# Raw LoRA weights fetched two pieces ahead into a two-buffer tile, in a one-core hybrid RWKV-7 / FoX block

## The chip, the cores and the metric

The kernel runs on one core of one Trainium2 chip. The metric is the device time of one execution in microseconds (us). The kernel before took 854.08 us, the median of three runs (852.34, 854.08 and 855.10).

In the text, PE is TensorE (PEld its weight loads), DVE is VectorE, ACT is ScalarE, POOL is GpSimd, and SP is SyncE, whose queue issues nearly all loads. L501 is line 501 of the kernel before; in the kernel after, lines behind the change stand 13 further down (L795 becomes L808), those before it keep their numbers.

## The reference, cut to what matters

One layer on 528 tokens (16 learned ones put ahead of 512) of width 1024. All is float32; the kernel splits each projection operand into a rounded high part and a low rest and multiplies in three passes.

```python
u = rmsnorm(h, norm_mix[l])
proj = u @ w_in[l]                       # 1024 x 5384: RWKV-7 features, FoX features, gates
...
r, k, v, wd, ad, gd = jnp.split(f, ...)  # f: RWKV-7 features after the token shift
w_log = -jax.nn.softplus(-(w0 + jnp.tanh(wd) @ w_lora_up)) - DECAY_OFFSET
decay = jnp.exp(-jnp.exp(w_log))
a = jax.nn.sigmoid(a0 + ad @ a_lora_up)
g = jax.nn.sigmoid(gd) @ g_lora_up
...
y = wkv7_scan(r, decay, k, v, -kk, kk * a_h)     # delta rule, per head of 64
...
return (y + bonus) * g
...
merged = gates_A * (y_rw @ w_out_rw) + gates_B * (y_fx @ w_out_fx)
h = h + merged @ w_o
z = rmsnorm(h, norm_mlp)
h = h + square(relu(z @ w_up)) @ w_down
```

The change concerns the loads of `w_lora_up`, `a_lora_up` (64 x 512 each) and `g_lora_up` (128 x 512).

## The kernel before

**The stages.** The opening (to about 54 us) loads the tokens transposed, forms the norm's sums of squares, computes the two low-rank blocks of the projection (L304, blocks `B_LORA` and `B_GD`) on tokens that are not yet scaled, and then writes the scaled tokens back into their high and low parts `uhi` and `ulo` (L398, L400, L401). The mixed stage (to about 415 us) runs four streams against each other: the RWKV-7 recurrence, FoX attention, FoX features, and the 40 blocks of the projection (L501) that fill PE between the others' steps. Then come the output projections (L1058, L1090, L1107) and the MLP (L1137, L1255).

**How the order is made.** In the mixed stage a planner (`Turns`, with `Clock` as its model of the engines) walks the streams and writes out PE's order, which is kept as written. DVE, ACT, POOL and SP get their order from the tile scheduler: it takes instructions by priority, and an instruction only once its tile has a free buffer. The recurrence's instructions are issued at high priority, so the scheduler may place a load or a conversion far ahead of where the program has it, if its buffer is free. Each engine then works strictly through its own order; the SP queue too, so a load that waits for its buffer holds every load behind it.

**The LoRA pieces.** The low-rank weights come in eight pieces of 128 x 128 float32 (64 KB): for each of four pairs of heads p, part 0 (decay and rate, used at L720 by `pup`) and part 1 (gate, used at L972 by `pg`). `load_lora` (L678) asks for a raw piece, converts it on ACT (L270, `lw0`), and forms the low rest on DVE (L271, `lw1`). Part 0 of a pair is asked for when `decay` of that pair starts, part 1 of both pairs of a group when `chain` of that group starts. The raw tile `lraw` shares the tag `yT` and its one buffer with four other tiles: `rkb` (L773), `tmp` of the inverse (L826), `yT` of the group norm (L962), and every other `lraw`. A piece's load can so be issued only when the last reader of that buffer is done.

**What lies near it.** `inverse` (L804) inverts the chunks' triangular blocks: a long run of small DVE operations through `tmp` (L830, L831), transposes (L833, L834), then PE products `pw` (L845) that DVE turns into `AX` (L851, L856) and `Tt` (L857). Right behind it stand the part-1 pieces of the chain. The small PSUM tiles (`pw`, `psc`, `pup`, `pkk`, `psr` and others) share four banks. `psc` are attention scores (L611), which DVE reads at L620 and L622. `keys` (L732) squares the keys on ACT (L737), sums them on PE (`pkk`, L741), and goes on through DVE and ACT to the scores `psr` (L794).

Of the kernel before, what the change touches and what calls it, by code (L numbers as in the profile page):

```python
# [9 lines left out]
F32 = mybir.dt.float32  # L10
# [176 lines left out]
def kernel(ctx, tc, ht, x, win, par, cst, gain, lora, wout, wo, wup, wdn, out, dbg=None):  # L187
    nc = tc.nc
# [80 lines left out]
    def split(hi, lo, x):  # L269
        A.copy(hi, x)  # L270
        V.tensor_tensor(lo, x, hi.bitcast(F32), ALU.subtract)  # L271
# [8 lines left out]
    with ExitStack() as st:  # L280
# [28 lines left out]
        rp = st.enter_context(tc.tile_pool(name="rp", bufs=1))  # L309
# [364 lines left out]
        def pad(t):  # L674
            G.memset(t[:, :PADT], 0.0)
            return t[:, PADT:]

        def load_lora(p, part, bufs):  # L678
            raw = rp.tile([128, 128], F32, name="lraw", tag="yT")
            nc.sync.dma_start(raw, lora[p][:, 128 * part:128 * part + 128])  # L680
            lw = [wp.tile([128, 128], F32R, name=f"lw{part}{i}", bufs=bufs) for i in range(2)]
            split(lw[0], lw[1], raw)
            return lw

        normalised = [[Event(), Event()] for g in range(2)]

        class Pair:
# [20 lines left out]
            def decay(self):  # L708
                p = self.p
                lw = load_lora(p, 0, 1)  # L710

                self.sg = sg = rp.tile([128, TP], F32, name="sg")
                self.tha = rp.tile([128, TP], F32, name="tha")
                dst = [pad(sg), pad(self.tha)]
                for a0, a1 in ((0, HT), (HT, T)):
                    yield lambda: max(ck.ready(*lw), banks(2))
                    pos = [psm("pup")[:, :HT] for i in range(2)]
                    for n, (wi, xi) in enumerate(((0, 0), (0, 1), (1, 0))):
                        for po, hs in zip(pos, hss):
                            mm(po, lw[wi][hs], (lhi, llo)[xi][hs, 0, a0:a1], start=n == 0, stop=n == 2)  # L720
                    for i in range(2):
                        tanh(dst[i][:, a0:a1], pos[i], bias=prh[:, i, p:p + 1], scale=0.5)
                V.tensor_scalar(dst[0], dst[0], 0.5, 0.5, ALU.mult, ALU.add)
                self.lc = lc = rp.tile([128, TP], F32, name="lc")
                V.tensor_tensor_scan(lc, smask.rearrange("p a b -> p (a b)"), sg, 0.0, ALU.mult, ALU.add)
                self.P = P = rp.tile([128, NCH, 64], F32, name="P")
                act(P.rearrange("p a b -> p (a b)"), lc, AF.Exp, scale=-CDEC)
                act(lc, lc, AF.Exp, scale=CDEC)
                self.pend = rp.tile([128, NCH], F32, name="pend", bufs=4)
                V.tensor_copy(self.pend, P[:, :, 63])  # L730
# [147 lines left out]
        def chain(g, prs):  # L878

            y = y_rw[:, 2 * g:2 * g + 2, :].rearrange("p a (b c) -> p a b c", c=64)  # L880
            lws = [load_lora(2 * g + pr_, 1, 2) for pr_ in range(2)]

            def ppy(name):
# [154 lines left out]
    with ExitStack() as st:  # L1038
# [37 lines left out]
        for j in range(2):  # L1076
            we = yp.tile([128, 2, 2, 512], F32R, name=f"we{j}", tag=("y_rw", "y_fx")[j])
            for x in range(2):
                raw = wp.tile([128, 512], F32, name="wraw", bufs=4)
# [11 lines left out]
        for k in range(KB):  # L1091
            raw = wp.tile([128, 512], F32, name="wraw", bufs=4)
# [293 lines left out]
```

## Time and profile before

| | |
|---|---|
| median of three runs | 854.08 us (852.34 to 855.10) |
| the profiled execution: its own time | 852.02 us |
| its span in the profile | 850.2 us, so 1.8 us lie outside it |
| granted TensorE clock | 0.998 over the span |
| PE busy | 827.5 us (97%) |
| DVE busy | 618.1 us (73%) |
| ACT busy | 454.0 us (53%) |
| POOL busy | 133.5 us (16%) |
| DMA | 95.88 MB, mean 113 GB/s |

How to read it: a timeline's row gives the start, the busy time from the first start to the last end, engine, line, operation, the tile written and the tiles read, the form and a count; in brackets stands how long the engine had been idle before it, and what ended that. Starts one after the other on a busy engine are closer than the busy times, since an instruction's end overlaps the next one's start. The list of waits has, for an engine and line, the line waited for, the total, the number of waits and the longest. PE's busy time is not PE at its peak: ends of matmuls are modelled.

### The profile page before, as it was taken

How to read it: one execution, taken by the hardware profiler on the slowest of the kernel's cores; microseconds unless marked ns; L12 is line 12 of the kernel's file. 1: busy time of each engine (PE TensorE's matmuls, PEld its weight loads, DVE VectorE, ACT ScalarE, POOL GpSimd, SP SyncE). 2: the span in 40 equal slices, each digit the busy share in tenths (PEclk: the TensorE clock that was granted, in tenths of full speed). 3: DMA queues.
4: the chain of work that ended last, by engine and by line, in shares of the span. 5: the costliest groups of instructions: out<-in, count | busy, mean ns of one | idle time of the engine just before them, and what ended most of it. 6: DMA issues, size and time to landing. Idle time of an engine off the chain costs nothing.

```text
span 850.2 us, 15285 instructions
## 1 busy us (share of the span) xinstructions
PE 827.5 (97%) x5740; PEld 679.1 (80%) x5740; DVE 618.1 (73%) x1222; ACT 454.0 (53%) x923; POOL 133.5 (16%) x133
## 2 busy tenths in 40 slices
PE   7999989999999999999999999999999999999998
PEld 6888977878887787677788779888888888888886
DVE  6996976679867876566357564877787677768788
ACT  7857536765656337654465442664355435534452
POOL 1041300003012000000012101203700560055000
PEclk9999999999999999999999999999999999999999
DMA  6132231111222212123386432651743274346421
GB/s 225 52 103 59 64 122 43 39 55 36 71 93 82 80 58 89 39 87 100 120 286 221 151 103 75 195 165 50 240 157 99 78 250 132 87 130 192 119 93 74
DMA packets 51338, 95.88 MB, mean 113 GB/s; under 512 B 5816, under 2 KB 6968, under 8 KB 51264
## 3 DMA queue, kind: packets, MB, share of 16 engines
q1 hardware_dynamic: 47680, 86.52, 32.0%
q0 software_dynamic: 1280, 4.20, 1.6%
q10 hardware_dynamic: 2304, 4.20, 1.5%
q8 instruction: 45, 0.74, 0.4%
q14 instruction: 29, 0.24, 0.1%
HBM read 88.57 MB, written 6.31 MB: 112 GB/s over the span
## 4 chain that ended last, share of the span: by engine, by line
PE 78%; DVE 10%; DMA 5%; ACT 3%; issue 3%; POOL 1%; SPq 0%; DVEq 0%; ACTq 0%; POOLq 0%
PE pj L501 24%; PE po L1137 21%; PE po L1255 12%; PE pd L1255 5%; DMA gl<-gd 2%; PE po L1107 2%; PE psc L611 1%; PE pw L845 1%; DVE wlo L471 1%; DMA wraw<-in_wo 1%; PE py L656 1%; PE ppt L640 1%; DVE wlo L236 1%; PE psr L794 1%; PE pch L905 1%
## 5 line engine op out<-in xcount | busy, mean ns | idle before, releaser
L501 PE MATMUL pj<-uhi,whi 128*128 128x264 f32 (+1 forms) x480 | 165.9, 346 | 0.0
L501 PE MATMUL pj<-ulo,whi 128*128 128x264 f32 (+1 forms) x480 | 154.3, 321 | 1.4 <-DVE ulo L401 1.4
L501 PE MATMUL pj<-uhi,wlo 128*128 128x264 f32 (+1 forms) x480 | 154.3, 321 | 0.0
L501 PEld LDWEIGHTS pj<-uhi,whi 128*128 128x128 f32 x480 | 90.3, 188 | 15.0 <-issue 6.7
L236 DVE TENSOR_TENSOR wlo<-wraw,whi 128x512 fp32r<-128x512 f32 x88 | 70.4, 809 | 38.2 <-ACT whi L235 35.9
L501 PEld LDWEIGHTS pj<-ulo,whi 128*128 128x128 f32 x480 | 90.6, 189 | 8.2 <-issue 1.7
L501 PEld LDWEIGHTS pj<-uhi,wlo 128*128 128x128 f32 x480 | 90.4, 188 | 7.2
L1137 PE MATMUL po<-zhi,whi 128*128 128x512 f32 (+1 forms) x248 | 94.8, 382 | 0.0
L1137 PE MATMUL po<-zlo,whi 128*128 128x512 f32 (+1 forms) x248 | 94.8, 382 | 0.0
L1137 PE MATMUL po<-zhi,wlo 128*128 128x512 f32 (+1 forms) x248 | 94.8, 382 | 0.0
L235 ACT CAST whi<-wraw 128x512 fp32r<-128x512 f32 x88 | 53.8, 617 | 51.4 <-DMA wraw<-in_wup 23.3
L471 DVE TENSOR_TENSOR wlo<-wraw,whi 128x512 fp32r<-128x512 f32 x80 | 61.3, 773 | 17.3 <-ACT whi L470 16.9
L470 ACT CAST whi<-wraw 128x512 fp32r<-128x512 f32 x80 | 48.9, 617 | 35.1 <-PE pj L501 33.8
L270 ACT CAST whi<-t 128x512 fp32r<-128x512 f32 x64 | 39.9, 624 | 44.4 <-DVE wlo L271 20.6
L271 DVE TENSOR_TENSOR wlo<-t,whi 128x512 fp32r<-128x512 f32 x64 | 49.3, 782 | 18.9 <-ACT whi L270 18.0
L1255 PE MATMUL po<-wlo,fhi 128*128 128x512 f32 x160 | 62.7, 392 | 0.2 <-DVE wlo L271 0.2
L1255 PE MATMUL po<-whi,flo 128*128 128x512 f32 x160 | 62.3, 390 | 0.0
L1255 PE MATMUL po<-whi,fhi 128*128 128x512 f32 x160 | 61.9, 389 | 0.0
L1183 POOL TENSOR_TENSOR t<-traw 128x512 f32<-128x512 f32 x24 | 34.9, 1462 | 155.1 <-DVE wlo L271 136.0
L1137 PEld LDWEIGHTS po<-zlo,whi 128*128 128x128 f32 x248 | 46.6, 188 | 9.1
L1137 PEld LDWEIGHTS po<-zhi,wlo 128*128 128x128 f32 x248 | 46.6, 188 | 9.0
L1137 PEld LDWEIGHTS po<-zhi,whi 128*128 128x128 f32 x248 | 46.6, 188 | 9.0
(307 smaller groups left out, 1754.8 us busy)
## 6 DMA issues: line engine op xcount, KB each, us to landing
wraw<-in_win SPq DMA_DIRECT2D x84, 256.0 KB, 2.6
wraw<-in_wup SPq DMA_DIRECT2D x64, 256.0 KB, 3.4
wraw<-in_wdn SPq DMA_DIRECT2D x48, 256.0 KB, 2.7
traw<-in_wdn SPq DMA_DIRECT2D x48, 256.0 KB, 3.0
gd<-gt ACTq DMA_DIRECT2D x16, 256.0 KB, 2.2
wraw<-in_wout SPq DMA_DIRECT2D x16, 256.0 KB, 3.1
gl<-gd SPq DMA_DIRECT2D x16, 256.0 KB, 3.2
wraw<-in_wo SPq DMA_DIRECT2D x16, 256.0 KB, 3.5
```

What stands on the lines that cost most here:

```text
L235: A.copy(hi, raw)
L236: low.tensor_tensor(lo, raw, hi.bitcast(F32), ALU.subtract)
L270: A.copy(hi, x)
L271: V.tensor_tensor(lo, x, hi.bitcast(F32), ALU.subtract)
L470: A.copy(hi, raw)
L471: low.tensor_tensor(lo, raw, hi.bitcast(F32), ALU.subtract)
L501: mm(po, a, b[:, k, a0:a1], start=n == 0, stop=n == 23)
L611: mm(sc, q[hs, 128 * i:128 * i + 128], k[hs, a:b], start=True, stop=True)
L1107: mm(po, a[:, k, 128 * i:128 * i + 128], b[:, k, :], start=n == 0, stop=n == 23)
L1137: mm(po[:, t0:t1], a, b[:, k, t0:t1], start=n == 0, stop=n == 23)
L1183: eng.tensor_tensor(t, sums[c, pair] if c in (T1, T2) else c, d, ALU.add)
L1255: mm(x[i], a[:, k, left, 128 * i:128 * i + 128], c, start=start and k == 0 and n == 0, stop=stop and k == n_pairs - 1 and n == 2)
```

## The change

The raw pieces get a tile of their own, `lraw` with two buffers, and no longer share `yT`. A list `lora_line` names the eight pieces in the order of their use. Two are fetched before the streams start, and `load_lora`, which now only takes the piece that was fetched, asks for the next one in the list behind its own conversion. The conversions themselves, the destinations (`lw`: one buffer for part 0, two for part 1), and the computation stay.

```diff
+        lora_line = [(0, 0), (1, 0), (2, 0), (0, 1), (1, 1), (3, 0), (2, 1), (3, 1)]
+        lora_raws = {}
+
+        def fetch_lora():
+            if lora_line:
+                p, part = lora_line.pop(0)
+                raw = rp.tile([128, 128], F32, name="lraw", bufs=2)
+                nc.sync.dma_start(raw, lora[p][:, 128 * part:128 * part + 128])
+                lora_raws[p, part] = raw
+
+        fetch_lora()
+        fetch_lora()
+
         def load_lora(p, part, bufs):
-            raw = rp.tile([128, 128], F32, name="lraw", tag="yT")
-            nc.sync.dma_start(raw, lora[p][:, 128 * part:128 * part + 128])
+            raw = lora_raws.pop((p, part))
             lw = [wp.tile([128, 128], F32R, name=f"lw{part}{i}", bufs=bufs) for i in range(2)]
             split(lw[0], lw[1], raw)
+            fetch_lora()
             return lw
```

The number and kinds of the instructions are the same on every engine; only places move. PE's order differs in one place: the first two `pup` products stand five matmuls later, behind the end of the `B_GD` block. The first two fetches are no longer issued from within a high-priority stream.

The start of SP's queue. In the kernel before, the first raw piece stands ahead of all other loads and the second between the third and the fourth chunk of tokens:

```order
L680 DMA lraw_469<-in_lora 128x128
L337 DMA pr_64<-in_par 128x133
L339 DMA xt0_116<-in_ht 128x528 x3
L680 DMA lraw_861<-in_lora 128x128
L339 DMA xt0_116<-in_ht 128x528
L232 DMA wraw_123<-in_win 128x512
```

In the kernel after, SP begins with the parameters and the tokens, and the first two pieces follow the constants `cs`; a third stands among the projection's weights:

```order
L337 DMA pr_64<-in_par 128x133
L339 DMA xt0_116<-in_ht 128x528 x4
L232 DMA wraw_123<-in_win 128x512
...
L344 DMA cs_63<-in_cst 128x576
L685 DMA lraw_467<-in_lora 128x128
L685 DMA lraw_469<-in_lora 128x128
L457 DMA wraw_483<-in_win 128x512
L457 DMA wraw_485<-in_win 128x512
L457 DMA wraw_495<-in_win 128x512
L685 DMA lraw_477<-in_lora 128x128
```

What moved: two loads of 64 KB from ahead of the tokens to behind the constants.

DVE in the middle of the inverse of the first group, kernel before: the low rest of the piece (1, 1) (`lw11`) stands between the low rests of the projection's weights (`wlo`) and the first readers of `pw` (L851):

```order
L471 TENSOR_TENSOR wlo_1531<-wraw_1496,whi_1530 128x512
L471 TENSOR_TENSOR wlo_1657<-wraw_1534,whi_1656 128x512
L271 TENSOR_TENSOR lw11_1876<-lraw_1873,lw10_1875 128x128
L851 TENSOR_TENSOR AX0_1319<-pw_1551,cs_63 128x384
L851 TENSOR_TENSOR AX0_1319<-pw_1565,cs_63 128x384
L851 TENSOR_TENSOR AX0_1319<-pw_1579,cs_63 128x384
```

The same place after (L851 is now L864):

```order
L471 TENSOR_TENSOR wlo_1535<-wraw_1500,whi_1534 128x512
L471 TENSOR_TENSOR wlo_1661<-wraw_1538,whi_1660 128x512
L864 TENSOR_TENSOR AX0_1323<-pw_1555,cs_63 128x384
L864 TENSOR_TENSOR AX0_1323<-pw_1569,cs_63 128x384
L864 TENSOR_TENSOR AX0_1323<-pw_1583,cs_63 128x384
```

What moved: the conversions of (2, 0), (0, 1) and (1, 1), which stood within ten rows here on DVE and ACT, are gone from this place.

They stand in or soon behind the opening instead. DVE at the end of the opening, kernel after: the pieces (0, 1) (`lw11_1872`) and (1, 1) (`lw11_1878`) stand between the last low parts of the tokens (L401) and the keys' token shift (L318 `okk`):

```order
L401 TENSOR_TENSOR ulo_97<-xt1_117,uhi_96 128x2x264
L271 TENSOR_TENSOR lw11_1872<-lraw_869,lw10_1871 128x128
L743 COPY pend_541<-P_538 128x9
L401 TENSOR_TENSOR ulo_97<-xt1_117,uhi_96 128x2x264
...
L318 SCALAR_TENSOR_TENSOR okk_511<-pj_543,pr1_65,tm_513 128x264
L271 TENSOR_TENSOR llo_104<-lf1_110,lhi_103 128x528
L271 TENSOR_TENSOR lw11_1878<-lraw_1865,lw10_1877 128x128
L318 SCALAR_TENSOR_TENSOR okk_511<-pj_570,pr1_65,tm_513 128x264
```

Before, no LoRA piece stands between these:

```order
L401 TENSOR_TENSOR ulo_97<-xt1_117,uhi_96 128x2x264
L418 TENSOR_SCALAR lf1_110<-lf1_110 128x528
L471 TENSOR_TENSOR wlo_496<-wraw_491,whi_495 128x512
L471 TENSOR_TENSOR wlo_500<-wraw_493,whi_499 128x512
L271 TENSOR_TENSOR llo_104<-lf1_110,lhi_103 128x528
L318 SCALAR_TENSOR_TENSOR okk_507<-pj_539,pr1_65,tm_509 128x264
L318 SCALAR_TENSOR_TENSOR okk_507<-pj_566,pr1_65,tm_509 128x264
```

What moved: two conversions into this stretch, on DVE as shown and on ACT alike. The piece (0, 0), which DVE converted among its first instructions before, now follows the low rests of the `B_GD` weights; (2, 0) comes some 50 rows behind the opening; (3, 0) keeps its place; (2, 1) and (3, 1) move ahead from the second group's inverse into the second stretch of group norm of the first group.

## The prediction

> **What bounds the kernel now.** I read first the page's head, then PE's list of waits.
>
> ```profile
> span 850.2 us, 15285 instructions
> PE 827.5 (97%) x5740; PEld 679.1 (80%) x5740; DVE 618.1 (73%) x1222; ACT 454.0 (53%) x923; POOL 133.5 (16%) x133
> ...
> PE pss L360 <- ACT sq L352: 5.7, 1, 5.7
> PE psc L611 <- DVE AX L851: 2.4, 1, 2.4
> PE po L1058 <- ACT yhi L270: 1.6, 1, 1.6
> PE pj L501 <- DVE ulo L401: 1.4, 1, 1.4
> ...
> PE pup L720 <- ACT sg L255: 0.7, 1, 0.7
> ```
>
> PE is idle for 850.2 − 827.5 = 22.7 us in all, so a change that leaves PE's work alone can gain only where one of these gaps closes. Which of them hang on a LoRA load? The view of the tile `lraw` lists what engines waited for:
>
> ```profile
>   DMA lraw<-in_lora: 15.2, 6
>   ACT lw L270: 7.2, 3
> ...
> DMA to landing us min/median/max: 1.7/1.9/3.2
> ```
>
> ACT waited 15.2 us for six raw pieces, and DVE 7.2 us for ACT's part of three. That is a large wait of two engines in strict order; what PE saw of it is another matter, and the timelines tell it. First ACT, DVE, then PE, in the inverse of the first group:
>
> ```profile
> 116.14 0.30 ACT L270 CAST lw<-lraw 128x128 fp32r<-128x128 f32 x1 [2.91 <-DMA lraw<-in_lora]
> 116.34 0.62 ACT L470 CAST whi<-wraw 128x512 fp32r<-128x512 f32 x1
> 120.00 0.30 ACT L270 CAST lw<-lraw 128x128 fp32r<-128x128 f32 x1 [3.04 <-DMA lraw<-in_lora]
> 122.16 0.62 ACT L470 CAST whi<-wraw 128x512 fp32r<-128x512 f32 x1 [0.76 <-DVE wlo L471]
> 126.11 0.30 ACT L270 CAST lw<-lraw 128x128 fp32r<-128x128 f32 x1 [3.33 <-DMA lraw<-in_lora]
> ...
> 122.81 0.69 DVE L471 TENSOR_TENSOR wlo<-wraw,whi 128x512 fp32r<-128x512 f32 x1 [0.67 <-ACT whi L470]
> 126.43 0.29 DVE L271 TENSOR_TENSOR lw<-lraw,lw 128x128 fp32r<-128x128 f32 x1 [2.93 <-ACT lw L270]
> 126.64 1.48 DVE L851 TENSOR_TENSOR AX<-pw,cs 128x384 f32<-128x384 f32 x3
> ...
> 124.31 0.51 PE L611 MATMUL psc<-ka,qa 64*128 64x144 f32 x2
> 127.25 0.51 PE L611 MATMUL psc<-ka,qa 64*128 64x144 f32 x2 [2.43 <-DVE AX L851]
> ```
>
> The three pieces come one behind the other through one buffer: load, ACT, DVE, next load. The third reaches DVE at 126.43, and DVE, in order, holds L851 behind it, though `pw` had left PE long before. The second pair of `psc` needs a PSUM bank that L851 frees; PE stands for 2.43 us. Of the other waits for `lraw` one pair is in the second group's inverse:
>
> ```profile
> 298.64 0.30 ACT L270 CAST lw<-lraw 128x128 fp32r<-128x128 f32 x1 [2.44 <-DMA lraw<-in_lora]
> 303.30 0.30 ACT L270 CAST lw<-lraw 128x128 fp32r<-128x128 f32 x1 [2.87 <-DMA lraw<-in_lora]
> ```
>
> No gap of PE lies there: its list names none for this place, and the stretch from 300 us reads
>
> ```profile
> 300.00:350.00 50.00, 50.00 (x690) 39.00 (x690) 30.14 (x82) 27.20 (x76) 0.00 (x0) 1.00 0.20 67
> ```
>
> that is, 50.00 us of PE in 50.00. These 5.3 us of ACT are hidden, and I count nothing for them.
>
> **The change part by part.** The computation and PE's work are the same; three places matter.
>
> *The inverse of the first group.* The three conversions leave. DVE's L851 then follows `wlo` of 122.81, which ends at 122.81 + 0.69 = 123.50; one of three L851 takes 1.48 / 3 = 0.49 us, so the first bank is free near 124.0. PE has the first `psc` pair at 124.31 and would start the second some 0.25 us later: the whole 2.43 us goes. What is late next? The second and third L851 end near 125.0, and PE needs their result behind the second `psc` pair, near 125.0 too. I take the full 2.43 us, and as the lower end 1.2 us, half, for this close meeting and for what follows in step with it (`pup` behind ACT's `sg`, 0.7 us, in the list above, is a chain of ACT alone and moves along). The upper end is 2.9 us, DVE's own 2.93.
>
> *The head of SP's queue.* Two loads of 64 KB leave the place ahead of the tokens:
>
> ```profile
> 0.74 0.38 SPq L680 DMA_DIRECT2D lraw<-in_lora  x1
> 1.18 0.42 SPq L337 DMA_DIRECT2D pr<-in_par  x1
> 1.65 1.37 SPq L339 DMA_DIRECT2D xt<-in_ht  x3
> 3.30 0.33 SPq L680 DMA_DIRECT2D lraw<-in_lora  x1
> 3.67 0.43 SPq L339 DMA_DIRECT2D xt<-in_ht  x1
> ...
> 4.96 0.64 ACT L352 ACTIVATE sq<-xt 128x528 f32<-128x528 f32 x1 [1.65 <-DMA xt<-in_ht]
> ```
>
> The parameters and tokens start 1.18 − 0.74 = 0.44 us earlier, and so do the squares at 4.96 on which PE's first 5.7 us wait. ACT and PE have no other wait of that size in the next 10 us, so the opening's work starts 0.44 us earlier. Whether PE keeps all of it depends on its cold stretch, which two rows show:
>
> ```profile
> 5.66 5.18 PE L360 MATMUL pss<-sq,ones 128*128 128x264 f32 x12 [5.66 <-ACT sq L352]
> ...
> 17.35 3.72 PE L360 MATMUL pss<-sq,ones 128*128 128x264 f32 x16
> ```
>
> The same product's passes take 5.18 / 12 = 0.43 us at first and 3.72 / 16 = 0.23 us later. [...]
>
> *The conversions in the opening.* There the earlier start meets an engine that has no room:
>
> ```profile
> 30.00:40.00 10.00, 8.60 (x69) 7.71 (x68) 9.94 (x21) 9.30 (x21) 0.28 (x2) 1.00 0.21 72
> ...
> 35.18 0.27 DVE L271 TENSOR_TENSOR lw<-lraw,lw 128x128 fp32r<-128x128 f32 x1
> 35.38 0.42 DVE L723 TENSOR_SCALAR sg<-sg 128x528 f32<-128x528 f32 x1
> ...
> 38.11 1.93 DVE L401 TENSOR_TENSOR ulo<-xt,uhi 128x528 fp32r<-128x528 f32 x3
> ...
> 38.86 0.39 PE L501 MATMUL pj<-ulo,whi 128*128 128x264 f32 x1 [1.39 <-DVE ulo L401]
> ...
> 44.17 0.74 ACT L737 ACTIVATE sq<-okk,pr 128x528 f32<-128x528 f32 x1
> ...
> 44.96 1.16 PE L741 MATMUL pkk<-sq,cs 128*128 128x264 f32 x4
> ```
>
> DVE is busy 9.94 us of 10 and ACT 9.30. A conversion costs a full engine the step to its next start: 35.38 − 35.18 = 0.20 us on DVE, 116.34 − 116.14 = 0.20 us on ACT. Three of them are new ahead of the keys' squares at 44.17: (0, 0), which sat in DVE's empty first 3 us, (0, 1) and (1, 1). That is 0.60 us later against 0.44 us earlier: +0.16 us. PE waits for the squares (44.17 + 0.74 = 44.91, and `pkk` starts at 44.96), so whatever PE gains ahead of that, the 1.39 us at 38.86 included, is lost again here. The L401 order in the new kernel (two of the four late chunks now ahead of the scan) shortens that wait at 38.86, but the squares decide. I take +0.2 us for the opening.
>
> Its bounds. Below: −0.44 us, if the conversions find room. Above: ACT and DVE would wait if (0, 1) and (1, 1) have not landed. The load of (0, 1) is issued behind DVE's conversion of (1, 0), near 35.5; with the median 1.9 us it lands at 37.4. ACT comes to it only behind `P`, which the following row puts at 37.30 + 0.68 = 37.98:
>
> ```profile
> 37.30 0.68 ACT L727 ACTIVATE P<-lc 128x576 f32<-128x576 f32 x1 [0.67 <-DVE lc L725]
> ```
>
> So 0.6 us of cover; with the longest landing, 3.2 us, ACT would stand 0.7 us, and as much again at (1, 1). Upper end: 0.2 + 1.4 = +1.6 us.
>
> *The rest.* SP gets new places where it can wait: a fetch stands behind the conversion that frees its buffer, and the projection's weights behind the fetch. Those weights themselves wait for `wlo` on DVE, which in each case stands within a few rows of that conversion, so the fetch costs them one issue, 0.33 us, against blocks of PE work of several us. (3, 0) keeps its place. (2, 0) goes to DVE near 71 us, ahead of a wait that takes it up:
>
> ```profile
> 74.29 0.49 DVE L318 SCALAR_TENSOR_TENSOR okk<-pj,pr,tm 128x264 f32<-128x264 f32 x1 [2.43 <-ACT tm L317]
> ```
>
> (2, 1) and (3, 1) go to the group norm, where PE has no gap in the list that ends on them. I count 0 for these, with 0.3 us to either side.
>
> The sum, against the profiled execution of 852.02 us (span 850.2, 1.8 outside): −2.43 + 0.2 = −2.2 us, 849.8 us. The median of the runs is 854.08, 2.06 above that execution; against it the forecast is 854.08 − 2.2 = **851.9 us**.
>
> **The rivals.**
> - *The opening gains too* (chance 0.17). If DVE's places at 38 us leave the squares unhurt, the 0.44 us stays: −2.43 − 0.44 = −2.9 us, 851.2. For it: L401 of the first late chunks comes ahead of the scan. Against it: `pkk` waits for ACT, not for L401.
> - *Half of the gap comes back* (0.22). PE meets the second and third L851, or the inverse's later products, and gains 1.2 us, loses 0.2: 854.08 − 1.0 = 853.1. For it: the meeting near 125.0. Against it: DVE gains 2.9 where PE gains 2.4.
> - *Slower: the waits move to the opening* (0.08). If (0, 1) and (1, 1) come to ACT's turn before they have landed, ACT and DVE stand for each as they stood at 116 to 126, 2.9 to 3.3 us, but now in the stretch where they are full and PE has the 1.39 us gap: up to 6.2 − 2.4 = +3.8 us, 857.9. It decides as soon as the two waits pass 2.4 us together, that is, from a landing of 1.9 + 0.6 + 1.2 = 3.7 us each. Against it: the longest seen is 3.2.
> - *The gap was not the piece's* (0.08). If L851 would have waited anyway, nothing is gained: 854.1 to 854.5. Against it: `pw` had ended by 124.31, and DVE names ACT's `lw`.
>
> **How the numbers follow.** The forecast has 0.45, the rivals 0.17, 0.22, 0.08 and 0.08. A measurement of this kernel tells about 0.3% from no change, 2.56 us here, so faster means below 851.5 and slower above 856.6. The forecast lies 0.4 us above the first line, and the three runs lie up to 1.7 us from their median, so of its 0.45 I give 0.21 to faster and 0.24 to same. The first rival gives 0.13 and 0.04, the second 0.02 and 0.19 with 0.01 for slower, the slower one 0.06 for slower and 0.02 for same, the last 0.07 for same and 0.01 for slower. Faster 0.36, same 0.56, slower 0.08. The range reaches from the first rival less 1.5 us of scatter, 849.7, to the second with as much, 854.6.
>
> **What would show it.** Right: no row of `lw` with a wait for `lraw` between 110 and 130 us, L851 directly behind `wlo`, the second `psc` pair within 0.3 us of the first, PE's idle time down by 2 to 2.5 us. The opening's step is right if `pkk` starts within 0.3 us of 44.96, and wrong if it starts before 44.6 or behind 45.5. The forecast as a whole is wrong if ACT waits for `lraw` between 36 and 43 us, or if a new gap of over 1 us stands behind 125 us.

## The result, and the profile after

The changed kernel takes 848.5 us (median of four runs, 847.27 to 849.18) against 854.0 us (four runs, 852.34 to 855.1): a ratio of 0.9944, 95% interval 0.9927 to 0.996. The forecast was 851.9 us, between 849.7 and 854.6; the time lies 1.2 us below the range. The profiled execution of the changed kernel took 849.18 us, that of the kernel before 852.02: between these two the difference is 2.8 us, between the medians 5.5. Most of what follows is about that disagreement.

The head of the page and PE's list of waits, after:

```profile
span 847.4 us, 15278 instructions
PE 825.8 (97%) x5740; PEld 678.1 (80%) x5740; DVE 616.5 (73%) x1222; ACT 454.2 (54%) x923; POOL 135.1 (16%) x133
```

```profile
PE pss L360 <- ACT sq L352: 4.9, 1, 4.9
PE pj L501 <- DVE ulo L401: 1.6, 2, 1.3
PE po L1071 <- ACT yhi L270: 1.6, 1, 1.6
PE ppt L638 <- DVE pe L627: 1.3, 1, 1.3
```

The wait of `psc` is gone from PE's list. PE's first wait is 0.8 us shorter, and the wait for `ulo` has become two. The timeline of the first group's inverse, DVE and then PE (code behind the change stands 13 lines lower than before):

```profile
121.11 2.50 DVE L471 TENSOR_TENSOR wlo<-wraw,whi 128x512 fp32r<-128x512 f32 x4
...
123.52 1.49 DVE L864 TENSOR_TENSOR AX<-pw,cs 128x384 f32<-128x384 f32 x3
...
125.24 0.40 PE L501 MATMUL pj<-uhi,wlo 128*128 128x512 f32 x1
125.57 0.52 PE L611 MATMUL psc<-ka,qa 64*128 64x144 f32 x4
126.02 0.91 PE L858 MATMUL pw<-AX,Tt 64*64 64x64 f32 x24
```

`AX` follows `wlo` directly, all four `psc` go in one piece, and the next `pw` comes at 126.02, where it came at 127.71. From the first `psc` to that `pw` there are 126.02 − 125.57 = 0.45 us, before 127.71 − 124.31 = 3.40. In the opening, from the tokens to the keys' squares, the timelines of SP, ACT, DVE and PE read:

```profile
4.19 0.64 ACT L352 ACTIVATE sq<-xt 128x528 f32<-128x528 f32 x1 [1.31 <-DMA xt<-in_ht]
...
4.89 3.45 PE L360 MATMUL pss<-sq,ones 128*128 128x264 f32 x7 [4.89 <-ACT sq L352]
...
34.26 0.82 SPq L599 DMA_DIRECT2D nF<-fF_d  x2
...
35.39 0.27 DVE L271 TENSOR_TENSOR lw<-lraw,lw 128x128 fp32r<-128x128 f32 x1
35.69 5.64 SPq L685 DMA_DIRECT2D lraw<-in_lora  x2
...
40.35 0.30 ACT L270 CAST lw<-lraw 128x128 fp32r<-128x128 f32 x1 [1.73 <-DMA lraw<-in_lora]
40.68 0.29 DVE L271 TENSOR_TENSOR lw<-lraw,lw 128x128 fp32r<-128x128 f32 x1 [1.32 <-ACT lw L270]
...
40.96 0.70 DVE L401 TENSOR_TENSOR ulo<-xt,uhi 128x528 fp32r<-128x528 f32 x1
...
41.72 0.39 PE L501 MATMUL pj<-ulo,whi 128*128 128x264 f32 x1 [1.31 <-DVE ulo L401]
...
45.40 0.74 ACT L750 ACTIVATE sq<-okk,pr 128x528 f32<-128x528 f32 x1
...
46.19 1.16 PE L754 MATMUL pkk<-sq,cs 128*128 128x264 f32 x4 [0.69 <-ACT sq L750]
```

The start came 5.66 − 4.89 = 0.77 us earlier. Then the piece (0, 1), issued at 35.69 right behind two broadcasts of `nF`, landed only near 40.3, after 4.6 us. ACT stood 1.73 us for it, DVE 1.32 us, the last chunk of `ulo` waited behind it, and PE stood 1.31 us. `pkk` starts at 46.19, 1.23 us later than before. That is one pair of traces. Three traces of kernels with the opening of before have `pkk` at 44.28, 44.34 and 44.96 us, five with the opening of after at 45.64 to 46.91, on the mean 1.5 us later. The tile's own view agrees:

```profile
  ACT lw L270: 8.8, 4
  DMA lraw<-in_lora: 1.7, 1
...
DMA to landing us min/median/max: 1.7/2.0/4.9
```

So the same PE instruction, set side by side in the two traces, stands at −0.77 us at the start, +1.23 at `pkk`, −1.69 at the `pw` behind the gap. There is one more step, and no change in the program's order goes with it. In the windows from 277.0 to 280.5 us the columns behind the instruction counts are the granted clock, the DMA share and GB/s; first before, then after:

```profile
277.00:280.50 3.50, 3.50 (x36) 2.57 (x33) 1.77 (x4) 0.48 (x1) 0.00 (x0) 0.59 0.02 5
```

```profile
277.00:280.50 3.50, 3.50 (x21) 2.32 (x16) 3.26 (x6) 0.84 (x2) 1.25 (x2) 1.00 0.00 0
```

In the execution before, the clock is granted at half for a stretch of 3.41 us here (276.47 to 279.88, mean granted clock 0.50), and over it the distance between the same instructions of the two traces grows from 1.73 to 3.24 us, that is, by 1.5. The execution after has no such stretch. The two stay 3.2 us apart up to the output projections, where the execution after waits some 0.4 us more, and 2.8 us apart from there to the end.

### The profile page after: what moved, and what is told of

Same layout as the page of the kernel before. It is cut to its first block, busy times and chain, and to the rows that moved or that the text cites. A ratio compares the mean times of both kernels' runs of the same rounds, so it can differ in the third digit from the quotient of the medians.

```text
span 847.4 us, 15278 instructions
## 1 busy us (share of the span) xinstructions
PE 825.8 (97%) x5740; PEld 678.1 (80%) x5740; DVE 616.5 (73%) x1222; ACT 454.2 (54%) x923; POOL 135.1 (16%) x133
## 4 chain that ended last, share of the span: by engine, by line
PE 80%; DVE 5%; DMA 4%; ACT 4%; issue 2%; POOL 1%; SPq 0%; ACTq 0%; DVEq 0%; POOLq 0%
PE pj L501 25%; PE po L1150 21%; PE po L1268 12%; PE pd L1268 5%; DMA gl<-gd 2%; PE pw L858 2%; PE po L1120 2%; PE psc L611 1%; DMA wraw<-in_wo 1%; PE py L656 1%; PE ppt L640 1%; PE psr L807 1%; PE pssq L553 1%; PE pch L918 1%; PE pch L924 1%
```

## The experiments

**What is to be told apart.** Theory A: the gap of PE at 127.25 costs its own length and, beyond that, makes stretches at half clock more frequent, which the runs pay for and one profiled execution shows only by chance. Rival B: only waits count, and the stretches have nothing to do with the gap. Apart from that: which part of the change closed the gap, and what the opening's move is worth.

Each run is recorded with its mean granted clock. One stretch of 3.41 us at half takes 3.41 / 2 / 850 = 0.002 off the mean, so 0.998, 0.996 and 0.994 stand for about one, two and three stretches. Over all 186 runs of the ten kernels, with a constant for each kernel, 0.002 less of clock goes with 1.5 us more of time. In the table the last column is that constant: the time at a clock of 1.000. A single run scatters by about 1.2 us around this fit. Each mean also holds a tail at half clock behind the last matmuls, which costs nothing (in the execution after 0.51 over its last 1.1 us, with no matmul in them, and 0.999 over the span from this alone; in the execution before 0.51 over its last 0.3 us), so the numbers of stretches are on the high side, and differences are what to go by. The copies, own_tile and one_buffer ran on one chip; the last six kernels of the table ran on another, on which the kernel after was not run without an edit. The kernel before ran on both, at mean clocks of 0.9964 on the first and of 0.9964 and 0.9971, in two measurements, on the second. The ratios compare within one chip.

| kernel | runs | median us | ratio to before, 95% | mean clock | at 1.000, us |
|---|---|---|---|---|---|
| before, with its copy | 89 | 852.8 | 0.9997 [0.9981, 1.0013] (copy) | 0.9966 | 850.2 |
| after, with its copy | 13 | 848.8 | 0.9952 [0.9936, 0.9968] (copy) | 0.9992 | 848.2 |
| own_tile | 6 | 848.05 | 0.9945 [0.9926, 0.9965] | 0.9988 | 847.4 |
| one_buffer | 6 | 847.0 | 0.9931 [0.991, 0.9951] | 0.9982 | 845.7 |
| opening_only | 12 | 852.33 | 0.9985 [0.9966, 1.0003] | 0.9962 | 849.0 |
| first_two | 12 | 850.69 | 0.9971 [0.9957, 0.9985] | 0.9980 | 848.9 |
| gap_half | 12 | 852.93 | 1.0004 [0.9989, 1.002] | 0.9972 | 851.0 |
| gap_back | 12 | 855.18 | 1.0025 [1.0012, 1.0038] | 0.9954 | 851.7 |
| fill | 12 | 850.29 | 0.9981 [0.9967, 0.9996] | 0.9977 | 849.0 |
| fill_after | 12 | 851.41 | 0.9986 [0.9971, 1.0002] | 0.9974 | 849.4 |

**The two kernels once more**, without any edit, for their clocks. The kernel before:

> The kernel before, once more, to see how its executions scatter. In the two profiles the gap of 2.43 us at 127 us is gone and the opening is 1.2 us later, which with a half-speed stretch of the clock near 277 us that only the profile of before has makes 2.9 us; the medians differ by 5.5 us. Theory A: ordinary executions of the kernel before have one to three half-speed stretches of 3.4 us (about 1.7 us each), set off by PE's gaps, so the mean granted clock of its executions reads 0.996 to 0.998 and the longer an execution, the lower its clock, by about 1.7 us per 0.002. Theory B: executions scatter by 1 to 2 us for other reasons (landing times); then the clock reads 0.998 or more in all and does not go with the time. Either way a time of 852 to 855 us, ratio 1.00.

The kernel after:

> The kernel after, once more, beside the kernel before on the same chip. Theory A: clock 0.999 to 1.000 in nearly all executions, time 847 to 849.5 us, 5 us below before. Theory B: the first medians were a lucky draw; the difference falls back towards the 2.9 us of the two profiles, 850 to 851 us.

On one chip the copy of the kernel before took 852.96 us (twelve runs) at clocks of 0.995 to 0.998, the copy of the kernel after 848.91 us (nine runs) at 0.998 to 1.000. No run of the kernel before, 89 in all, was granted 0.999 or more; 11 of the 13 of the kernel after were. The copy of the kernel before has the gap at `psc` again, in its list of waits:

```profile
PE psc L611 <- DVE AX L851: 2.1, 1, 2.1
```

Its one stretch at half clock lies elsewhere this time, near 424 us; that of the copy of the kernel after lies near 64 us (both profiled executions were granted 0.998). Where the stretch falls changes from execution to execution, how many there are goes with the kernel. The stretches are not all that changes: from 470 to 510 us, in the output projections, PE is busy 38.25 us before, 39.97 in the copy and 37.91 after, so the waits there alone make up to 2.1 us between executions.

**The tile alone.** Only the raw tile gets its own two buffers; each load stays where the program had it.

```diff
-            raw = rp.tile([128, 128], F32, name="lraw", tag="yT")
+            raw = rp.tile([128, 128], F32, name="lraw", bufs=2)
```

> The kernel before with only the raw tile changed: two buffers of its own, every piece still asked for where it is used. The scheduler then places the loads as early as the buffers allow: as in the kernel after, but with the first two at the head of SP's queue. Theory: the tile of its own is the whole change but for the opening's start; the gap at 127 us is closed, the start is 0.5 to 0.8 us later than in the kernel after, (0, 0) is converted in the empty first 3 us, and the time is within 0.7 us of the kernel after, 848 to 849.5 us. Rival: fetching ahead is what brings the gain, and the time is nearer to the kernel before, 851 to 854 us.

It took 848.05 us, the time of the full change. The scheduler takes the loads early by itself as soon as they need not wait for `yT`. PE's rows, at the keys' squares and at the first group's inverse:

```profile
45.58 1.16 PE L741 MATMUL pkk<-sq,cs 128*128 128x264 f32 x4
...
124.17 0.52 PE L611 MATMUL psc<-ka,qa 64*128 64x144 f32 x4
124.61 0.91 PE L845 MATMUL pw<-AX,Tt 64*64 64x64 f32 x24
```

The gap is closed, and `pkk` comes 0.6 us earlier than with the full change. In the five traces with the opening of after, `pkk` stands between 45.64 and 46.91, so these 0.6 us are within their scatter. Asking two pieces ahead is thus not needed for the gain: two buffers of their own for the raw pieces suffice.

**One buffer.** The change with one buffer and one piece ahead.

```diff
-                raw = rp.tile([128, 128], F32, name="lraw", bufs=2)
+                raw = rp.tile([128, 128], F32, name="lraw", bufs=1)
...
-        fetch_lora()
```

> The kernel after with one raw buffer and one piece fetched ahead: pieces (0, 1) and (1, 1) are converted behind (2, 0), near 72 us, not in the opening. In the profile after, ACT waited 1.7 us at 40 us for (0, 1), which landed late, and the keys' sums pkk start 1.2 us later than before. Theory: that wait is the price of the opening, so here pkk starts 1 us earlier than in the kernel after, the gap at 127 us stays closed, and the time is 1 us less, 847 to 848 us. Rival: the later places on SP, ACT and DVE (a chain of load, conversion, load behind 71 us) bring waits of their own, and the time is that of the kernel after or more, 848.5 to 850 us.

At 847.0 us, as the expectation had it, it is the shortest of all, 1.9 us under the copy of the kernel after on the same chip (six runs of 845.95 to 848.42 against nine of 847.91 to 850.84). With one buffer (0, 1) and (1, 1) cannot be converted before (2, 0) is, near 66 us, and the opening is rid of them. Its `pkk`, and PE, PEld, DVE, ACT and POOL from 36 to 46 us, here and then in the kernel after:

```profile
43.58 1.16 PE L753 MATMUL pkk<-sq,cs 128*128 128x264 f32 x4
```

```profile
36.00:46.00 10.00, 9.56 (x70) 8.79 (x69) 9.30 (x20) 9.47 (x17) 2.02 (x3) 1.00 0.39 118
```

```profile
36.00:46.00 10.00, 7.92 (x61) 7.29 (x59) 8.36 (x19) 8.14 (x18) 0.14 (x1) 1.00 0.35 110
```

PE is busy 1.64 us more in these 10 us, and `pkk` comes 2.61 us earlier. By this pair of traces the opening lost 1.6 to 2.6 us to the two pieces, and it is recovered by letting them wait.

**The head of the queue alone.** The kernel before, in which only (0, 0) and (1, 0) come ahead through a tile of their own; the other six stay in `yT`.

```diff
+        ahead_raws = {}
+        for p in range(2):
+            raw = rp.tile([128, 128], F32, name="lahead", bufs=2)
+            nc.sync.dma_start(raw, lora[p][:, :128])
+            ahead_raws[p, 0] = raw
...
-            raw = rp.tile([128, 128], F32, name="lraw", tag="yT")
-            nc.sync.dma_start(raw, lora[p][:, 128 * part:128 * part + 128])
+            raw = ahead_raws.pop((p, part), None)
...
```

> The kernel before with the opening's part of the change alone: the first two pieces, (0, 0) and (1, 0), come through a tile of their own and leave the head of SP's queue; the other six are loaded as before, in the inverses. Theory: the start is 0.5 to 0.8 us earlier, (0, 0) costs DVE and ACT 0.2 us each in the full stretch, and (0, 1), whose late landing cost 1.7 us in the kernel after, is not there, so pkk starts 0.3 to 0.8 us earlier than before; the gap at 127 us and the clock of 0.995 to 0.998 stay; time 852.2 to 852.8 us against 853.0. Rival: the earlier start is eaten up at pkk, and the time is that of before within 0.2 us; then the whole gain of the change lies in the inverse.

852.33 us: the interval reaches from −2.9 to +0.3 us, so the runs leave open whether this part gains. In its trace PE's first product starts at 4.87 us, but `pkk` at 44.37 lies among the 44.28 to 44.96 of the traces with the old opening. The gap is still there, and the mean clock, 0.9962, is that of the kernel before:

```profile
126.39 0.51 PE L611 MATMUL psc<-ka,qa 64*128 64x144 f32 x2 [2.94 <-DVE AX L859]
```

**The other six ahead.** The first two pieces stay as before, the other six go through the list.

```diff
+        lora_line = [(2, 0), (0, 1), (1, 1), (3, 0), (2, 1), (3, 1)]
...
+            first = part == 0 and p < 2
+            if first:
+                raw = rp.tile([128, 128], F32, name="lraw", tag="yT")
...
```

> The other part alone: (0, 0) and (1, 0) are loaded as in the kernel before, through yT; the other six come ahead through a tile with two buffers, the first two of them at the head of SP's queue too, so that three loads of 64 KB stand ahead of parameters and tokens, and (0, 1) is converted in DVE's empty first 3 us. Theory: the gap at 127 us is closed (2.9 us, and the clock at 0.998 to 1.000); the start is 0.4 us later than before; no wait for (0, 1) at 40 us, so pkk is within 0.5 us of the kernel before; time 853.0 - 2.9 - 1 to 2 + 0.4 = 848.5 to 849.5 us, that of the kernel after. Rival: the late start passes to the end of the opening and beyond, 850 us.

850.69 us, more than the theory gave (848.5 to 849.5) and nearest to its rival's 850. The edit puts two more loads ahead of the tokens, as SP's and PE's rows show:

```profile
0.74 0.39 SPq L692 DMA_DIRECT2D lraw<-in_lora  x1
1.19 0.89 SPq L685 DMA_DIRECT2D lahead<-in_lora  x2
2.13 0.43 SPq L337 DMA_DIRECT2D pr<-in_par  x1
...
6.30 2.13 PE L360 MATMUL pss<-sq,ones 128*128 128x264 f32 x4 [6.30 <-ACT sq L352]
```

PE starts 1.41 us later than in the kernel after, but the rival's reason is not borne out: `pkk` stands at 45.61 and the `pw` behind the gap's place at 125.42, against 46.19 and 126.02 in the kernel after, and the gap is closed. What the run does say is on the clock: on this chip it is 0.9980 on the mean against 0.9964 of the kernel before. Why the median is 1.8 us above that of the kernel after, measured on the other chip, stays open; the fit puts 0.9 us of it to the clock.

**The gap put back.** The kernel after, with DVE multiplying the first `pw` of the inverse by 1.0 five times, or seven, ahead of `AX`. The values don't change; DVE is late by a known amount, and PE stands again.

```diff
+                if g == 0 and b0 == 0:
...
+                    for _ in range(5):
+                        V.tensor_scalar(p1, p1, 1.0, None, ALU.mult)
...
```

> The same with five such operations: a gap of about 1.5 us. Theory A: whether a stretch of half speed is set off depends on how empty PE is over some us, so a shorter gap sets it off less often: clock between that of the kernel after and that of the longer gap, time 848.9 + 1.5 + 0 to 1 = 850.4 to 851.4 us. Theory B: 850.4 us and the clock of the kernel after.

> The kernel after, with a stall put back into the first group's inverse that has nothing to do with LoRA: the first pw tile is multiplied by 1 in place seven times on DVE (about 0.5 us each) before L864 reads it. The computation is the same. PE gets a gap of about 2.5 us near 126 us. Theory A (PE's gap also costs clock): the time rises by more than the gap, since a half-speed stretch of 3.4 us comes with it in more than half of the executions: mean granted clock 0.996 to 0.998 where the kernel after has 0.998 to 1.000, time 848.9 + 2.5 + 1 to 2 = 852.4 to 853.5 us. Theory B (the gap costs itself): the clock stays at 0.998 to 1.000 and the time is 851.4 us, plus or minus 0.5.

Five gave 852.93 us, seven 855.18 us, both more than the expectations allowed. The timeline of PE with five:

```profile
127.58 1.03 PE L858 MATMUL pw<-AX,Tt 64*64 64x64 f32 x24 [2.08 <-DVE AX L869]
128.35 1.54 PE L858 MATMUL pw<-Tt,AX 64*64 64x64 f32 x24
...
130.41 0.63 PE L501 MATMUL pj<-ulo,whi 128*128 128x512 f32 x1
130.84 0.63 PE L501 MATMUL pj<-uhi,wlo 128*128 128x512 f32 x1
...
132.14 0.40 PE L501 MATMUL pj<-uhi,whi 128*128 128x512 f32 x1
```

And windows of PE there, in which the column behind the count is the granted clock:

```profile
120.00:125.00 5.00, 5.00 (x86) 1.00 0.59 175
125.00:128.00 3.00, 0.93 (x19) 1.00 0.43 150
128.00:131.50 3.50, 3.50 (x45) 0.53 0.02 5
131.50:135.00 3.50, 3.50 (x76) 0.98 0.24 71
```

This is theory A in one execution. The gap is 2.08 us, about the size that the kernel before has. PE is busy 0.93 us of three, and the 3.5 us behind it are granted 0.53: matmuls take 0.63 us that take 0.40 afterwards. Against the kernel after, PE is 0.58 us early ahead of the gap, 1.56 us late behind it and 3.09 us late behind the half-clock stretch: 2.14 us for the gap and 1.53 for the stretch. It stays 3.1 us late up to 480 us. With seven multiplications, the wait and then the windows:

```profile
PE pw L858 <- DVE AX L869: 3.5, 1, 3.5
```

```profile
125.00:128.00 3.00, 0.56 (x5) 1.00 0.27 94
128.00:131.50 3.50, 2.44 (x46) 0.64 0.02 5
```

The gap is 3.5 us, a stretch follows again, and this execution has a second one near 280 us. A gap of 0, 2.1 and 3.5 us gives 848.8, 852.9 and 855.2 us: 4.1 and 6.4 us more, nearly twice the gap's length each time. Rival B gives 2.1 and 3.5. The first of these times is from the other chip; by the ratios to the kernel before, each within its chip, it is 4.4 and 6.2 us, with about 1 us either way from the scatter of the runs. The mean clock with seven, 0.9954, is below that of every kernel without the gap on its chip (0.9974 to 0.9980); with five, 0.9972 does not stand out from them.

PE's windows ahead of the stretch with five multiplications, and then, in the kernel before, up to the end of its gap and behind it:

```profile
124.82:128.23 3.41, 1.33 (x28) 1.00 0.41 139
```

```profile
123.84:127.25 3.41, 0.98 (x6) 1.00 0.78 244
127.25:130.66 3.41, 3.41 (x56) 1.00 0.10 28
```

PE is busy for 39% of the first and 29% of the second, and only the first has a stretch behind it: one follows a gap of 2.08 us here, and none the 2.43 us of the kernel before. The stretch at 276.47 us of the kernel before stands behind 3.42 us in which PE is busy 1.96 us, 57% (273.05 to 276.47). So how thinly PE was busy just ahead does not decide by itself whether a stretch follows; what does, these runs do not show.

**The gap filled, not closed.** If theory A holds, useless work in the gap should make the kernel before faster. Eight matmuls are written into the bank of the first `psc`, which the true product then overwrites; no other instruction changes its place.

```diff
-                            sc = psm("psc")[:, :b - a]
+                            bank = psm("psc")
+                            if p == 0 and i == 0 and e == 0:
...
+                                for _ in range(8):
+                                    mm(bank, uhi[:, 0, :128], uhi[:, 0, :512], start=True, stop=True)
...
+                            sc = bank[:, :b - a]
```

> The kernel before, with eight matmuls more (128x512, into the bank of the first psc, which the true product then overwrites; the order of all other instructions is unchanged). They stand on TensorE just ahead of the gap of 2.1 to 2.4 us at L611 and should take about 8 x 0.23 = 1.85 us of it, while the vector engine's AX, for which the second psc waits, comes when it came. So TensorE is busy in the gap, and nothing waits any less. Theory A (the gap costs its own length, and beside that raises the number of stretches of 3.41 us in which the clock is granted at half): the wait's length stays paid, but the stretches fall from about 1.8 an execution, as the granted clocks of 0.994 to 0.998 in the runs of the kernel before say, towards the 0.5 of the changed kernel, at about 1.5 us each: 852.9 - 1.3 x 1.5 = about 851 us (850.5 to 851.9), granted clocks mostly 0.997 and above. Rival B (the stretches have nothing to do with the gap, and only the wait counts): as before, 852.9 us, within 0.5, granted clocks of 0.994 to 0.998 as before.

And the same eight in the kernel after, as a control:

> The control to the run with eight matmuls ahead of the gap: the same eight in the changed kernel, which has no gap there. Where TensorE itself sets the time in that stretch they cost their 8 x 0.23 = 1.85 us, 848.9 + 1.85 = 850.8 us (theory A and rival B alike); where the vector engine's inverse sets it, less, down to nothing, 848.9 us.

The filled kernel took 850.29 us against 852.25 for the kernel before on the same chip, 0.3 to 2.8 us less by the interval, with eight matmuls more. Nothing waited less, as PE's timeline shows:

```profile
119.86 2.31 PE L851 MATMUL pw<-AX,Bm 64*64 64x64 f32 x72
...
123.59 2.01 PE L614 MATMUL psc<-uhi 128*128 128x512 f32 x8
125.53 0.51 PE L617 MATMUL psc<-ka,qa 64*128 64x144 f32 x2
126.62 0.51 PE L617 MATMUL psc<-ka,qa 64*128 64x144 f32 x2 [0.58 <-DVE AX L857]
127.08 0.91 PE L851 MATMUL pw<-AX,Tt 64*64 64x64 f32 x24
```

From the first `pw` to the one behind the gap there are 127.08 − 119.86 = 7.22 us; before, in a row of its timeline, that first `pw` starts at 120.48 and the other at 127.71, 7.23 us (6.94 in its copy). The wait is as long as it was, only its emptiness is gone. Rival B had no change within 0.5 us; the near end of the interval, 0.3 us, still lies inside that, so this run speaks against B and does not refute it alone. Nor is the size clear: against the kernel before in the same measurement the clocks rose from 0.9971 to 0.9977 on the mean, within their scatter and worth 0.5 us, and the median fell by 2.0. Where the other 1.5 us would come from is open.

The control took 851.41 us, 2.6 above the kernel after where 1.85 was expected, so the eight matmuls stand on the path there, as they should. Its clocks, 0.9974, are lower than those of the kernel after, which theory A did not foresee: its profiled execution, granted 0.995, has stretches near 63 and 425 us. The gap near 125 us is thus one cause of stretches and not the only one; whether the other chip has a part in the lower clocks was not tested.

One count sums up the traces. Five profiled executions have a gap of 2 us or more near 125 us (before, its copy, opening_only, gap_half, gap_back); three of them have a half-clock stretch directly behind it (opening_only, gap_half and gap_back, granted 0.55, 0.53 and 0.64 from 128.0 to 131.5 us). Of the seven without that gap (after, its copy, own_tile, one_buffer, first_two, fill, fill_after) none has one there. And on either chip the mean clock rose wherever the gap was closed: from 0.9964 to 0.9990 (the copy of the kernel after), 0.9988 and 0.9982 on one, from 0.9964 to 0.9980 on the other.

## Why the prediction was wrong

**What bounds the kernel, and the gap.** Right: the gap was the piece's, and it went, as foreseen in each sign (no row of `lw` there, `AX` directly behind `wlo`, `psc` in one piece). I counted −2.43 us, the idle time before the second pair. The traces give −1.69 − 1.23 = −2.92, close to my upper end of 2.9. The difference is in how the row counts: the two pairs started 127.25 − 124.31 = 2.94 us apart, and the next `pw` follows the start of four `psc` in one go after 0.45 us, as it followed the start of a single pair after 127.71 − 127.25 = 0.46. So the whole 2.94 were to be had, and not the idle time alone.

**The head of the queue.** 0.44 us were forecast, and 0.77 came at the first product. Of these 17.35 − 16.88 = 0.47 were left at the start of the last block of `pss`. Two executions of the kernel before differ by more there (17.35 and 16.70), so it is luck that 0.47 is near 0.44. In opening_only nothing of it is seen at `pkk`. By the clock records of the two traces the full clock starts at 10.23 us before and at 10.05 after: 0.18 us earlier, where the first product came 0.77 earlier.

**The conversions in the opening.** Mis-sized: forecast +0.2, measured +1.23 at `pkk`, or +1.5 on the mean of the eight traces. The step that failed is "with the median 1.9 us it lands at 37.4". It landed near 40.3, after 4.6 us, beyond the longest landing of 3.2 us that I had seen. My upper end of +1.6 held it. I had named the two signs (ACT waiting for `lraw` between 36 and 43 us, `pkk` behind 45.5); both came. This is the slower rival's mechanism in small: one wait of 1.73 us of ACT instead of two of about 3.

**The sum.** −2.92 + 1.23 = −1.7 us up to 128 us, where I had −2.2. By its own terms the forecast promised half a microsecond too much, and still the time came out 3.4 us lower than said.

**The step that failed** is the last one: "The median of the runs is 854.08, 2.06 above that execution; against it the forecast is 854.08 − 2.2". I took these 2.06 us for a constant that the change leaves alone, so the sum had no term for the clock. They were two things. Some 1.3 us are the draw of three runs, 854.08 against a median of 852.8 over 89 later ones. The rest goes with half-clock stretches, and these the change does not leave alone. The profiled execution had one of them (the 0.59 at 277 us), and by their clocks the runs of the kernel before had some 1.7 on the mean, those of the kernel after 0.4. That is (0.9992 − 0.9966) / 0.002 x 1.5 = 1.9 us beside the 1.7 that the instructions moved, together 3.6 of the 4.0 us between the medians of all runs (852.8 and 848.8). The remaining 0.4 is within the scatter. The 5.5 us of the first measurement, on four runs each, has an interval of 3.4 to 6.2 us and needs no further cause. So of the 3.4 us by which the forecast missed, 1.3 are the draw of the starting point and 0.3 that of the result; the other 1.8 are the missing term for the clock, 1.9, and the 0.4 within the scatter, less the 0.5 by which the forecast's own terms promised too much. How much of the clock's 1.9 us hangs on the gap alone, the runs do not say.

What in the profile could have told me? I quoted the cold stretch at the start, and looked at the clock there alone. The page's 0.998 over the span was in my table; with PE at 97% that says that some stretch ran slow, 0.002 x 850.2 = 1.7 us short of the full clock. Looking for it would have led to 277 us and to the question of what else empties PE for 2 us; the gap of 2.43 us that I wanted closed was the longest wait of PE in the mixed stage. The range was too narrow below for the same reason: it took the scatter of the three runs as noise, though the change acts on a part of what makes it.

**The rivals.** "The opening gains too" is the nearest by its number (851.2), and its reason is wrong. "Half of the gap comes back" did not happen: no new wait followed. No rival had the clock.

## What to carry to other kernels

Where the median of the runs lies above the profiled execution, ask what the profiled one was spared, above all when some stretch of it ran at a lower clock (here 0.50 for 3.41 us), and whether three runs are enough for a median, before adding the difference to a forecast as a constant. A gap of 2.08 us in a busy TensorE here cost 4.1 us, nearly twice its length (gap_half), so it is worth closing; that filling it pays is likely here, and not settled. And a transfer asked for earlier is converted earlier too: here the version with less lookahead, which kept the conversions out of the full opening, was the faster one (847.0 us against 848.9).

## What the runs showed of the hardware

The granted clock was 0.50 for 3.41 us in the kernel before (276.47 to 279.88), behind 3.42 us in which PE was busy 1.96, and 0.53 from 128.0 to 131.5 us in gap_half, behind 3.41 us in which PE was still busy 1.33; each of these stretches cost 1.5 us. Whether one comes differs between executions of one program too: the twelve runs of gap_half were granted 0.994 to 0.998. Three of the five executions with the gap near 125 us had one directly behind it; the kernel before, with PE busy 0.98 us of the 3.41 up to the end of its gap, had none there, and what decides it is not shown. And a load of 64 KB that takes 1.7 us at its quickest and 2.0 in the median took 4.6 us when issued 1.4 us behind the first of two broadcast loads of 264 KB in the same queue. That it was these two that held it back was not tested by itself; the first piece of the kernel after, issued at 8.2 us with no broadcast near it, took 4.9 us.
